# Moving columns of the down and output products read from two runs in turn

## The chip, the core and the metric

The kernel runs on one core of a Trainium2 chip. The time is the device time of one launch in microseconds (us). The core's engines work side by side and wait for each other through semaphores: TensorE (matmuls, PE in the profile; its loads of the stationary operand are PEld), VectorE (DVE), ScalarE (ACT), GpSimd (POOL) and SyncE (SP), which issues nearly all transfers.

## The reference

Two layers over 512 tokens of width 1024. Layer 0 mixes tokens by causal average pooling, layer 1 by stick-breaking attention with 16 heads of 64; each is followed by a squared-ReLU MLP of width 4096, and each block sits between two RMSNorms. Keys and values are projected once, after layer 0.

```python
def sq_relu_mlp(h, w_up, w_down):
    u = jnp.matmul(h, w_up)
    return jnp.matmul(jnp.square(jax.nn.relu(u)), w_down)
...
for layer in range(DEPTH):                      # DEPTH = 2
    h = rms_norm(x, mix_pre_g[layer])
    if layer < N_A:                             # layer 0
        m = pool_mixer(h, pool_w[layer], pool_scale[layer])
    else:                                       # layer 1
        q = ...matmul(h, w_q[j])...
        o = stick_breaking_attention(q, k, v)
        m = jnp.matmul(o..., w_o[j])            # the output projection
    x = x + rms_norm(m, mix_post_g[layer])
    h = rms_norm(x, mlp_pre_g[layer])
    x = x + rms_norm(sq_relu_mlp(h, w_up[layer], w_down[layer]), mlp_post_g[layer])
    if layer == N_A - 1:
        kv = jnp.matmul(rms_norm(x, kv_norm_g), w_kv)...
return x
```

`w_down` (the down projection, 4096 x 1024 in each layer) and `w_o` (the output projection, 1024 x 1024) are the two weights of the change.

## The kernel before

A matmul instruction has a stationary operand of 128 x 128, loaded by an instruction of its own, and a moving operand of 128 rows by up to 512 columns; one result column per moving column goes to a bank of PSUM (128 x 512 float32).

Every dense product is made of three matmuls. Each operand is split into a high part, rounded to the type float32r, and a low part, the remainder (`split`, or `weight` for weights that come from memory; ScalarE makes the high part and VectorE the low one). Then high x high, high x low and low x high are summed in PSUM (`mm3`). In the profile float32r operands of matmuls are listed as f32. The pooling's products (L769, L793) and the transposes on TensorE (L366, L827, L1025) are plain float32, without a split.

Where the products of the change lie:

- The up projection (`up_block`, L654 to L656) has the weights as stationary operand and the 512 tokens' activations, `xnh` and `xnl`, as moving one. Query and key projections go through it as well.
- The down projection has the activations as stationary operand and the weights as moving one, 512 columns at a time, half of the width of 1024. Its rows (4096, as 32 tiles of 128) come in five groups of 2, 3, 3, 3 and 3 pairs of tiles and a rest of 4 tiles.
- A group (class `Seven`) is a 2 x 2 block product done with seven products instead of eight: tokens are halved, rows are taken as even and odd tiles, and the output columns are halved (`NS`: 0 to 511 and 512 to 1023). `right` forms sums and differences of weight quarters on VectorE, in float32 and column by column, and splits them into a tile `w`; `left` does the same for the activations, into a tile `a`. `product` (L543) runs the matmuls, with `a` stationary and `w` moving, and VectorE or ScalarE adds each bank to `y` (L552, L549).
- `contract` multiplies plainly with `mm3` (L293 to L295). It does the rest of 4 tiles (weights named `dn`, or `w` where a pool lends a tile) and the output projection (weights `w`, the last one `h` and `l`; activations `ohl`). Its moving operands are halves of 512 columns too; only for the last 128 tokens of the last layer is the second half cut in two of 256 (`cuts`).
- The value projection (`values`) also uses `mm3`, with 256 moving columns.

The weights lie in memory as 128 x 1024 tiles, `in_wdn` and `in_wo`, arranged by the host program before the launch (`arrays` at the end of the program). The weights of attention are split into parts early and kept in memory (`kept`), to be fetched later.

The order of work: a scheduler places instructions that are not in a hand-made order; in layer 0's mixing, in scores, and in `contract` where a norm follows, the order on TensorE is the order of the code.

Of the kernel before, what the change touches and what calls it, by code (L numbers as in the profile page):

```python
# [15 lines left out]
P = 128  # L16
D = 1024
# [4 lines left out]
NJ = FF // P  # L22
# [6 lines left out]
PAIRS = HEADS // 2  # L29
WINDOWS = (2, 4, 8, 16)  # L30
EPS = 1e-6
TS = [slice(t * P, (t + 1) * P) for t in range(T)]
NS = [slice(0, 512), slice(512, 1024)]
# [38 lines left out]
def trunk(ctx, tc, x, consts, gcol, grow, pw, wup, wdn, wq, wk, wv, wo, out):  # L72
# [14 lines left out]
    def ps():  # L87
        return psum.tile([P, 512], F32, tag="ps", name=name("ps"))
# [145 lines left out]
    def fill(n=1):  # L234
        if gate[0]:
            behind.update(latest)
        for _ in range(n):
            if queue and len(made) < ahead and (queue[0][0][0] != "dn" or dn_pool[0]):
                make()
# [6 lines left out]
    for l in range(2):  # L246
        if l == 1:
            n = len(queue)
# [37 lines left out]
    def rstd(st, col, total=None):  # L286
# [2 lines left out]
        latest["pool"] = nc.gpsimd.tensor_tensor(out=r, in0=total, in1=mhalf, op=ALU.pow)  # L289
        return r  # L290

    def mm3(dst, ah, al, bh, bl, start, stop):
        nc.tensor.matmul(dst, ah, bh, start=start, stop=False)  # L293
        nc.tensor.matmul(dst, ah, bl, start=False, stop=False)  # L294
        nc.tensor.matmul(dst, al, bh, start=False, stop=stop)  # L295
# [9 lines left out]
    class Update:  # L305
# [24 lines left out]
        def product(self, n):  # L330
            return self.beside if n and self.cuts is not NS else self.scaled
# [46 lines left out]
    def contract(lhs, w, y, first, update=None, tiles=range(T), soon=False):  # L378


        last = len(lhs) - 1
        ups = {}
        for t in tiles:
            up = ups[t] = update(t, y[t]) if update is not None else None
            cuts = up.cuts if up is not None else NS
            pds = [ps()[:, : cut.stop - cut.start] for cut in cuts]

            def product(n, cs):
                for c in cs:
                    (lh, ll), (wh, wl) = lhs[c], w[c]  # L390
                    mm3(
                        pds[n], lh[:, TS[t]], ll[:, TS[t]], wh[:, cuts[n]], wl[:, cuts[n]],
                        c == 0, c == last,
                    )

            def evacuate(n):
                part = y[t][:, cuts[n]]
                if first:
                    nc.scalar.copy(part, pds[n])
                else:  # L400
                    nc.vector.tensor_tensor(out=part, in0=pds[n], in1=part, op=ALU.add)
                if up is not None:
                    up.square(n, part, nc.vector if n else nc.gpsimd)

            normed = up is not None and not up.final
            if t == 0:
                product(0, range(last))
                product(1, range(last))
                product(0, [last])
            else:  # L410
                product(0, range(last + 1))
            if normed and t == T - 1 and not soon:
                ups[0].transpose()
            evacuate(0)
            if normed and t > 0:
                ups[t - 1].rstd()
                behind_sum = soon and t == T - 1
                if not behind_sum:
                    ups[t - 1].norm()
            if t == 0:  # L420
                product(1, [last])
            elif normed and t == T - 1:
                product(1, [0])
                ups[1].transpose()
                product(1, range(1, last + 1))
            else:
                product(1, range(last + 1))
                if normed and soon and t == 2:
                    ups[0].transpose()
            evacuate(1)  # L430
            for n in range(2, len(cuts)):
                product(n, range(last + 1))
                evacuate(n)
            if up is None:
                fill()
            else:
                up.add(ups[t - 1].norm if normed and t > 0 and behind_sum else None)
                if normed and t == T - 2:
                    behind.update(latest)
        if normed:  # L440
            ups[T - 1].rstd()
            ups[T - 1].norm()
            for t in (T - 2, T - 1):
                pending[t] = ups[t]
# [4 lines left out]
    class Seven:  # L449
# [84 lines left out]
        def product(self, i, y, first):  # L534
            a, w = self.operands.pop(i)
            at, _, _, tokens, half = self.PRODUCTS[i]
            start = at not in self.banks
            if start:
                self.banks[at] = [ps(), ps()]
            for t, bank in enumerate(self.banks[at]):  # L540
                for q in range(self.n):
                    for k, (x, z) in enumerate(((0, 0), (0, 1), (1, 0))):
                        nc.tensor.matmul(  # L543
                            bank, a[:, x, q, TS[t]], w[:, z, q], start=start and q == 0 and k == 0,
                            stop=q == self.n - 1 and k == 2, skip_group_check=True,
                        )
                part = y[2 * tokens + t][:, NS[half]]
                if first and (tokens, half, t) not in first:
                    nc.scalar.copy(part, bank)  # L549
                    first.add((tokens, half, t))  # L550
                else:
                    nc.vector.tensor_tensor(out=part, in0=bank, in1=part, op=ALU.add)  # L552
# [322 lines left out]
    with tc.tile_pool(name="att", bufs=1, reuse_waits="tile") as ap:  # L875
        att_pool[0] = ap

        def values(u, part):
            if u not in vs:
                w = [get(("v", u, h)) for h in range(2)]  # L880
                vs[u] = w, ap.tile([P, T, 4, 2, HD], F32R, tag="v", bufs=2, name=name("v"))
            w, v = vs[u]
            for s in part:
                need(s)
                pv = ps()
                for k in range(KC):
                    c = slice((k % 4) * 256, (k % 4) * 256 + 256)
                    mm3(
                        pv[:, :256], xnh[:, k, TS[s]], xnl[:, k, TS[s]],
                        w[k // 4][0][:, c], w[k // 4][1][:, c], k == 0, k == KC - 1,  # L890
                    )
                pv4 = pv[:, :256].rearrange("p (h d) -> p h d", h=4)
                nc.scalar.copy(v[:, s, :, 0, :], pv4)
                nc.vector.tensor_tensor(
                    out=v[:, s, :, 1, :], in0=pv4, in1=v[:, s, :, 0, :].bitcast(F32), op=ALU.subtract
                )
# [22 lines left out]
        half = [slice(0, HD), slice(HD, P)]  # L919
# [249 lines left out]
```

## Time and profile before

| | |
|---|---|
| median of 3 timed runs | 946.29 us (946.13 to 946.48) |
| span of the profiled execution, first to last instruction | 944.4 us |
| granted TensorE clock, mean | 0.998 of full speed |
| TensorE busy with matmuls | 935.6 us (99%), 4762 matmuls |
| TensorE busy with loads of stationary tiles | 795.8 us (84%) |
| VectorE, ScalarE, GpSimd busy | 704.5, 566.1, 89.1 us |
| moved by transfers | 169.36 MB, 49.8% of the time of 16 transfer engines |

For the profiled execution the span is the only time that is recorded. The timed runs are 1.7 to 2.1 us above it. A busy time is the time in which at least one instruction of that kind was running; matmuls overlap, so that the mean duration of one is longer than the step from one to the next.

In the order of time: the pooling layer lies up to about 33 us, the first MLP from there to about 366 us, attention with its projections to about 606 us, the second MLP from there to the end. Line numbers are those of the kernel before; in the kernel after, each is 6 higher from `mm3` on.

### The profile page before, as it was taken

How to read it: one execution, taken by the hardware profiler on the slowest of the kernel's cores; microseconds unless marked ns; L12 is line 12 of the kernel's file. 1: busy time of each engine (PE TensorE's matmuls, PEld its weight loads, DVE VectorE, ACT ScalarE, POOL GpSimd, SP SyncE). 2: the span in 40 equal slices, each digit the busy share in tenths (PEclk: the TensorE clock that was granted, in tenths of full speed). 3: DMA queues.
4: the chain of work that ended last, by engine and by line, in shares of the span. 5: the costliest groups of instructions: out<-in, count | busy, mean ns of one | idle time of the engine just before them, and what ended most of it. 6: DMA issues, size and time to landing. Idle time of an engine off the chain costs nothing.

```text
span 944.4 us, 12431 instructions
## 1 busy us (share of the span) xinstructions
PE 935.6 (99%) x4762; PEld 795.8 (84%) x4762; DVE 704.5 (75%) x762; ACT 566.1 (60%) x972; POOL 89.1 (9%) x86
## 2 busy tenths in 40 slices
PE   9999999999999999999999999999999999999997
PEld 7998888888888888988889898898888888888886
DVE  5856797987969756589586887854695876857856
ACT  6658979687874537576647553555544444444632
POOL 2100000000000014000000000311220300403003
PEclk9999999999999999999999999999999999999999
DMA  7444989698683423998625264433414143133102
GB/s 278 170 143 158 340 283 321 234 351 296 235 303 131 155 90 112 359 399 318 238 90 179 90 240 163 156 112 104 164 42 168 58 134 112 45 134 112 47 21 89
DMA packets 46929, 169.36 MB, mean 179 GB/s; under 512 B 4832, under 2 KB 5306, under 8 KB 46870
## 3 DMA queue, kind: packets, MB, share of 16 engines
q1 hardware_dynamic: 46722, 168.55, 49.8%
q8 instruction: 37, 0.61, 0.3%
q14 instruction: 22, 0.18, 0.0%
q10 hardware_dynamic: 148, 0.02, 0.0%
HBM read 128.71 MB, written 39.85 MB: 178 GB/s over the span
## 4 chain that ended last, share of the span: by engine, by line
PE 93%; DVE 3%; DMA 1%; POOL 1%; issue 1%; ACT 1%; POOLq 0%; DVEq 0%; ACTq 0%
PE ps L543 28%; PE ps L655 15%; PE ps L654 15%; PE ps L656 15%; PE ps L293 4%; PE ps L295 4%; PE ps L294 4%; PE ps L976 2%; PE ps L1035 2%; PE ps L1025 2%; PE ps L793 1%; PE ps L769 1%; DMA w<-kept 1%; DVE x L340 1%; PE ps L827 0%
## 5 line engine op out<-in xcount | busy, mean ns | idle before, releaser
L543 PE MATMUL ps<-w,a 128*128 128x512 f32 x1176 | 279.4, 389 | 0.0
L655 PE MATMUL ps<-xnl,w 128*128 128x512 f32 (+1 forms) x712 | 261.8, 368 | 0.1
L654 PE MATMUL ps<-xnh,w 128*128 128x512 f32 (+1 forms) x712 | 261.7, 369 | 0.0
L656 PE MATMUL ps<-xnh,w 128*128 128x512 f32 (+1 forms) x712 | 261.7, 368 | 0.0
L543 PEld LDWEIGHTS ps<-w,a 128*128 128x128 f32 x1176 | 220.8, 188 | 45.8
L655 PEld LDWEIGHTS ps<-xnl,w 128*128 128x128 f32 x712 | 134.3, 189 | 22.3 <-DVE xnl L273 0.5
L656 PEld LDWEIGHTS ps<-xnh,w 128*128 128x128 f32 x712 | 134.2, 189 | 22.1
L654 PEld LDWEIGHTS ps<-xnh,w 128*128 128x128 f32 x712 | 133.6, 189 | 21.9 <-ACT xnh L272 0.2
L552 DVE TENSOR_TENSOR y<-ps,y 128x512 f32<-128x512 f32 x124 | 83.8, 684 | 44.1 <-PE ps L543 44.1
L135 DVE TENSOR_TENSOR w<-raw,w 128x1024 fp32r<-128x1024 f32 x56 | 69.4, 1240 | 62.7 <-ACT w L133 62.6
L133 ACT CAST w<-raw 128x1024 fp32r<-128x1024 f32 x56 | 58.8, 1050 | 79.9 <-PE ps L656 78.2
L328 POOL TENSOR_TENSOR y<-y,grow 128x512 f32<-128x512 f32 x12 | 18.7, 1562 | 576.0 <-ACT xn L276 576.0
L272 ACT CAST w<-e 128x1536 fp32r<-128x1536 f32 (+1 forms) x30 | 41.9, 1397 | 40.0 <-DVE e L516 27.1
L273 DVE TENSOR_TENSOR w<-e,w 128x1536 fp32r<-128x1536 f32 (+1 forms) x30 | 55.6, 1852 | 11.5 <-ACT w L272 11.2
L272 ACT CAST a<-r 128x768 fp32r<-128x768 f32 (+1 forms) x60 | 47.4, 790 | 25.7 <-DVE r L497 12.9
L273 DVE TENSOR_TENSOR a<-r,a 128x768 fp32r<-128x768 f32 (+1 forms) x60 | 59.2, 986 | 0.0
L1007 DVE TENSOR_TENSOR_SCAN e<-u,begin 128x1280 f32<-128x1280 f32 x16 | 45.2, 2822 | 17.4 <-ACT u L1001 16.9
L144 ACT ACTIVATE apart<-apart,gc 128x128 f32<-128x128 f32 (+1 forms) x136 | 43.7, 402 | 0.0
L272 ACT CAST w<-xn 128x1536 fp32r<-128x1536 f32 (+1 forms) x20 | 28.0, 1398 | 25.4 <-PE ps L543 25.4
L273 DVE TENSOR_TENSOR w<-xn,w 128x1536 fp32r<-128x1536 f32 (+1 forms) x20 | 33.0, 1651 | 13.3 <-ACT w L272 13.2
L273 DVE TENSOR_TENSOR w<-w,w 128x1536 fp32r<-128x1536 f32 (+1 forms) x20 | 34.6, 1731 | 9.4 <-ACT w L272 9.4
L272 ACT CAST w<-w 128x1536 fp32r<-128x1536 f32 (+1 forms) x20 | 28.0, 1400 | 21.0 <-PE ps L543 20.9
(151 smaller groups left out, 1418.5 us busy)
## 6 DMA issues: line engine op xcount, KB each, us to landing
w<-kept SPq DMA_DIRECT2D x70, 512.0 KB, 5.1
raw<-in_wup SPq DMA_DIRECT2D x62, 512.0 KB, 4.3
w<-in_wdn SPq DMA_DIRECT2D x8, 1536.0 KB, 7.0
kept<-wx SPq DMA_DIRECT2D x24, 512.0 KB, 4.9
xn<-in_wdn SPq DMA_DIRECT2D x8, 1536.0 KB, 6.5
kept<-apart SPq DMA_DIRECT2D x22, 512.0 KB, 5.0
kept<-xn SPq DMA_DIRECT2D x12, 512.0 KB, 8.1
kept<-spare SPq DMA_DIRECT2D x8, 512.0 KB, 5.3
```

Of the source, the lines that this page charges most:

```text
L133: nc.scalar.copy(hi, raw)
L135: nc.vector.tensor_tensor(out=lo, in0=raw, in1=hi.bitcast(F32), op=ALU.subtract)
L144: nc.scalar.mul(c, c, gc[:, lo + k : lo + k + 1])
L272: latest["act"] = nc.scalar.copy(hi, src)
L273: latest["dve"] = nc.vector.tensor_tensor(out=lo, in0=src, in1=hi.bitcast(F32), op=ALU.subtract)
L293: nc.tensor.matmul(dst, ah, bh, start=start, stop=False)
L543: nc.tensor.matmul(bank, a[:, x, q, TS[t]], w[:, z, q], start=start and q == 0 and k == 0, stop=q == self.n - 1 and k == 2, skip_group_che ...
L552: nc.vector.tensor_tensor(out=part, in0=bank, in1=part, op=ALU.add)
L654: nc.tensor.matmul(pu[:, cols], wh[:, k, :], xnh[:, k, cols], start=k == 0, stop=False)
L655: nc.tensor.matmul(pu[:, cols], wh[:, k, :], xnl[:, k, cols], start=False, stop=False)
L656: nc.tensor.matmul(pu[:, cols], wl[:, k, :], xnh[:, k, cols], start=False, stop=k == KC - 1)
L1007: nc.vector.tensor_tensor_scan(out=e[:, ::-1], data0=u[:, 1:][:, ::-1], data1=begin[:, ::-1], initial=0.0, op0=ALU.mult, op1=ALU.max,)
```

## The change

The host program permutes the columns of `w_down` and `w_o` within each half of 512: first the 256 even columns, then the 256 odd ones. A new helper, `by_twos`, views a half as two runs of 256 columns and takes one column from each in turn: position 0, 256, 1, 257 and so on, which are the columns in their natural order. `product` and `contract` give this view to TensorE as moving operand. So PSUM, and all that follows, holds the same columns as before; neighbouring columns of the moving operand lie 256 elements (1 KB) apart. For a cut of 256 columns the view takes 128 from each run.

Nothing else changes. Each engine has the same instructions in the same order as before, with the moving operand's pattern in the 1572 touched matmuls as the one difference, and each transfer moves the same shape.

```diff
+    def by_twos(w, cut):
+
+        half = w[:, NS[cut.start // 512]].rearrange("p (j i) -> p i j", j=2)
+        lo = cut.start % 512 // 2
+        return half[:, lo : lo + (cut.stop - cut.start) // 2]
+
     def mm3(dst, ah, al, bh, bl, start, stop):
...
                     mm3(
-                        pds[n], lh[:, TS[t]], ll[:, TS[t]], wh[:, cuts[n]], wl[:, cuts[n]],
+                        pds[n], lh[:, TS[t]], ll[:, TS[t]], by_twos(wh, cuts[n]), by_twos(wl, cuts[n]),
                         c == 0, c == last,
                     )
...
                         nc.tensor.matmul(
-                            bank, a[:, x, q, TS[t]], w[:, z, q], start=start and q == 0 and k == 0,
+                            bank, a[:, x, q, TS[t]], by_twos(w[:, z, q], NS[0]), start=start and q == 0 and k == 0,
                             stop=q == self.n - 1 and k == 2, skip_group_check=True,
                         )
...
+    twos = lambda w: w.reshape(*w.shape[:-1], 2, D // 4, 2).swapaxes(-1, -2).reshape(w.shape)
...
-        "wdn": a["w_down"].reshape(2, NJ, P, D),
+        "wdn": twos(a["w_down"].reshape(2, NJ, P, D)),
...
-        "wo": a["w_o"][0].reshape(PAIRS, P, D),
+        "wo": twos(a["w_o"][0].reshape(PAIRS, P, D)),
```

## The prediction

> **What bounds the kernel now.** I read the clock first, then the busy times and the waits, then the chain and the groups by shape, since the change touches only one operand of one kind of instruction. The core's clock, the page's spans, its chain by engine, and all that the trace lists as waits of TensorE:
>
> ```profile
> core 0: 944.4 us, clock 0.998
> span 944.4 us, 12431 instructions
> PE 935.6 (99%) x4762; PEld 795.8 (84%) x4762; DVE 704.5 (75%) x762; ACT 566.1 (60%) x972; POOL 89.1 (9%) x86
> PE 93%; DVE 3%; DMA 1%; POOL 1%; issue 1%; ACT 1%; POOLq 0%; DVEq 0%; ACTq 0%
> PE ps L700 <- POOL warm L662: 1.3, 1, 1.3
> PE ps L293 <- ACT xnh L272: 0.2, 1, 0.2
> ```
>
> The reader is to see a TensorE that never stands still: 935.6 of 944.4 us busy, 1.5 us of waits in all, at a granted clock of 0.998. So the time is a sum over matmuls, and what one matmul takes from its start to the next one's start goes straight into the result. The groups by shape show which are touched (names are output<-moving operand,stationary operand):
>
> ```profile
> L543 PE MATMUL ps<-w,a 128*128 128x512 f32 x1176 | 279.4, 389 | 0.0
> L293 PE MATMUL ps<-dn,sq 128*128 128x512 f32 x60 | 23.5, 392 | 0.0
> L293 PE MATMUL ps<-w,ohl 128*128 128x512 f32 x56 | 21.8, 398 | 0.0
> L293 PE MATMUL ps<-h,ohl 128*128 128x512 f32 x8 | 3.1, 390 | 0.0
> L293 PE MATMUL ps<-dn,sq 128*128 128x256 f32 x8 | 2.3, 282 | 0.0
> ```
>
> L543 is the seven-product part of both down projections. L293 is the first of the three matmuls of `mm3`; L294 and L295 have one for each of it. So 1176 + 3 x (60 + 56 + 8) = 1548 matmuls of 512 columns and 3 x 8 = 24 of 256 take their moving columns in the new way: 1572 matmuls, 1548 x 512 + 24 x 256 = 798,720 columns. The 389 ns of a row is no price, since matmuls overlap; the price is the step from start to start, which the chain of waits gives (start, us, what). Below are a run of L543, one of L793 (plain float32, 128x256) and one of L1025 (plain float32 transposes, 128 columns), then two rows of the timeline with 22 steps between them, all of 256 columns in the value projection, which the change leaves alone:
>
> ```profile
> 331.00 8.16 PE ps L543 x36
> ...
> 29.40 3.46 PE ps L793 x16
> ...
> 572.85 0.66 PE ps L1025 x6
> ...
> 366.86 0.28 PE L295 MATMUL ps<-w,xnl 128*128 128x256 f32 x1
> ...
> 369.50 0.28 PE L654 MATMUL ps<-xnh,w 128*128 128x256 f32 x1
> ```
>
> A step of 512 columns is 8.16 / 36 = 226.7 ns, one of 256 is 2.64 / 22 = 120.0 ns. The difference, 106.7 ns over 256 columns, is 0.4168 ns a column; what is left, 226.7 - 213.4 = 13.3 ns, is a fixed part of each matmul. The plain float32 rows give 3.46 / 16 = 216.3 ns for 256 columns and 0.66 / 6 = 110 ns for 128: 0.83 ns a column, twice as much, and a fixed part of only 216.3 - 2 x 0.4168 x 256 = 2.9 ns. Both kinds load a 128x128 float32 stationary tile for each matmul, so the load alone doesn't explain the 13.3 ns:
>
> ```profile
> L543 PEld LDWEIGHTS ps<-w,a 128*128 128x128 f32 x1176 | 220.8, 188 | 45.8
> L793 PEld LDWEIGHTS ps<-pw,yt 128*128 128x128 f32 x64 | 11.8, 190 | 1.9 <-issue 0.5
> ```
>
> **The change part by part.** *The moving operand.* It goes from one run of 512 elements to 256 pairs whose halves lie 1 KB apart. Nothing in this trace reads a moving operand in that manner, so the step of a touched matmul has to be bounded.
>
> From below: the whole fixed part goes. That is 13.3 ns x 1572 = 20.9 us, and 946.3 - 20.9 = 925.4 us. Less isn't excluded by any mechanism, but no row has a column cheaper than 0.4168 ns.
>
> From above: each column costs what it costs in the nearest slower rows, L793's, 0.83 ns. Then 0.4168 ns is added for each of 798,720 columns, 332.9 us, and 1279.2 us come out; 1262.8 us if the fixed part shrinks too, as it has in those rows.
>
> Which value? What sets fast from slow in the rows is the pace at which one run is read. At 0.4168 ns a column of one run, a matmul carries 13.3 ns beside its columns; at half that pace along a run, it carries 2.9 ns. After the change each of the two runs is read at half the pace, as L793's is, while together they would still give a column every 0.4168 ns. By that likeness a touched matmul of 512 columns takes 213.4 + 2.9 = 216.3 ns, and one of 256 takes 109.6 ns: 10.4 ns less each, 10.4 x 1572 = 16.4 us. I take this end, since L793 is the one group in which the fixed part is seen to be small with the same stationary loads; it is a likeness and no proof, because L793 differs also in how TensorE handles plain float32, and the chances below say so.
>
> [...]
>
> *The layout of the two weight tensors.* Nothing at run time: the columns are permuted within each half of 512 before the launch, the transfers have the same shapes and sizes, and the sums and differences of weight halves go column by column, so their instructions are the same. Order and number of instructions on all five engines stay as they are, SP's transfers among them.
>
> *What the shorter steps meet.* 588 of L543's matmuls lie in each layer, 6.1 us of gain in each of two stretches. The two stretches between the first and the last products of seven:
>
> ```profile
> core 0: us, PE busy (x) PEld busy (x) DVE busy (x) ACT busy (x) POOL busy (x), PEclk, DMA share, GB/s
> 62.90:338.00 275.10, 275.10 (x1215) 227.87 (x1214) 222.09 (x214) 208.97 (x347) 0.00 (x0) 1.00 0.70 249
> 607.80:920.00 312.20, 312.20 (x1463) 261.89 (x1463) 220.35 (x201) 152.63 (x186) 47.46 (x22) 1.00 0.30 101
> ```
>
> In the first VectorE is busy 222.1 of 275.1 us; in 269 it would be 83%, the DMA share 72%. The waits there point at TensorE, not from it:
>
> ```profile
> ACT w L272 <- PE ps L543: 59.1, 38, 2.2
> DVE y L552 <- PE ps L543: 44.1, 36, 4.2
> DVE e L516 <- DMA xn<-in_wdn: 10.1, 8, 2.1
> PEld ps L294 <- DMA w<-kept: 0.2, 1, 0.2
> ```
>
> VectorE and ScalarE wait 103 us for the touched matmuls, so they follow a faster TensorE at once. The cover that could go is the last row's: the kept output-projection weights land 0.2 us late once. But the slots they land in are freed by TensorE, so most of the transfer moves forward with it; I cost this at nothing, and at some 2 us if it stays where it is. The end of the chain stays as it is:
>
> ```profile
> 934.75 0.70 DVE y L401
> ...
> 936.34 1.57 POOL y L328
> ...
> 941.10 0.40 DVE x L340
> ```
>
> The last matmul's result is taken at 934.75 us, and what follows does not read the weights.
>
> *The sum.* The profiled execution's span is 944.4 us, 1.9 us under the median of the timed runs (946.29); that remainder lies outside the span and does not change. 944.4 - 16.4 = 928.0 us of span, and 946.3 - 16.4 = 929.9 us of time; I say 930.
>
> **The rivals.**
>
> *The column rate falls to half (slower).* Place: the reader of TensorE's moving operand, in all 1572 matmuls. If what it fetches from SBUF at a time serves only neighbouring columns, then alternating between two places makes each column a fetch of its own, and the rate is that of L793's rows. Price: 1262.8 to 1279.2 us, as above. It decides as soon as it adds more than 10.4 ns to a matmul, that is 25 column times in 512, one lost for every 20 columns. For it: all moving operands of the trace are contiguous, so nothing shows that two places can be kept open. Against it: nothing in the trace either; it is the open question. A cost between, some columns delayed and others not, would end between 948 and 1262 us.
>
> [...]
>
> *Nothing changes.* The 13.3 ns may belong to the exchange of the stationary tile at full column rate: in L793 that exchange has twice the time per column to hide in. If two runs are read as well as one, 226.7 ns stay, and the time is 946.3 us. For it: 512 and 256 columns show the same fixed part, as an exchange would. Against it: L793's 2.9 ns with the same loads.
>
> *Half the gain.* Only one of two starts of a run is hidden: 5.2 ns x 1572 = 8.2 us, 938 us.
>
> **How the numbers follow.** The full gain (near 930) gets 0.40 and the half gain 0.05; nothing changes 0.17; half the column rate 0.27; a cost in between 0.11. So faster 0.45, same 0.17, slower 0.38, where same means within 0.2% or 1.9 us, about what a measurement of this kernel can tell from no change. The likeliest case is the full gain, 930 us; its own range is 925 to 938. Cases of both signs hold most of the chance, so the whole range has to reach from 925 (the fixed part gone) to 1279 (each column doubled, the fixed part kept): leaving out the half rate would already leave out more than 2 in 10.
>
> **What would show it.** In the changed kernel, a run of 36 L543 matmuls (L549 there) should take 7.8 us in the chain instead of 8.16, with TensorE still at 99% and the up projections still at 226.7 ns. If such a run takes 8.16 us, the fixed part was not the reading's. If it takes about 15.5, the column rate has halved; then VectorE's and ScalarE's waits for L549 should grow to some hundred us, with their busy time unchanged. The forecast is wrong also if the steps shrink and the time does not: then a wait of TensorE for weights or operands must appear in its list, which has 1.5 us now.

## The result and the profile after

The changed kernel takes 932.55 us (median of 4 runs, 932.35 to 934.18) against 946.23 us of the kernel before on the same chip: a ratio of 0.9856, 95% interval 0.9842 to 0.9870. That is 13.7 us less, where the likeliest case of the forecast, 930 us, had 16.4 us less. The profiled execution took 932.74 us with a span of 930.9 us; the span of before was 944.4 us, so 13.5 us went.

From the page of the changed kernel, the span, the busy times and the chain by engine:

```profile
span 930.9 us, 12431 instructions
PE 921.5 (99%) x4762; PEld 797.6 (86%) x4762; DVE 703.6 (76%) x762; ACT 565.0 (61%) x972; POOL 91.7 (10%) x86
PE 93%; DVE 2%; DMA 1%; issue 1%; POOL 1%; ACT 1%; POOLq 0%; DVEq 0%; SPq 0%; ACTq 0%
```

TensorE is still the bound at 99%, and VectorE's and ScalarE's work is what it was (704.5 and 566.1 us before). All that went, went from TensorE's steps. The chain of waits of the changed kernel (start, us, what) has the run of 36 products that the prediction read at 331.00 us, and the end of the kernel:

```profile
326.58 7.77 PE ps L549 x36
...
921.22 0.70 DVE y L407
...
927.56 0.40 DVE x L346
```

7.77 / 36 = 215.8 ns a step, where 226.7 ns stood before. Two rows of its timeline, 16 steps apart in the last piece of 256 columns:

```profile
921.80 0.28 PE L300 MATMUL ps<-dn,sq 128*128 128x256 f32 x1
...
923.58 0.28 PE L301 MATMUL ps<-dn,sq 128*128 128x256 f32 x1
```

1.78 / 16 = 111 ns, 120.0 before. The groups by shape show what moved the other way (busy us, mean ns of one):

```profile
L549 PE MATMUL ps<-w,a 128*128 128x512 f32 x1176 | 266.6, 379 | 0.0
L660 PE MATMUL ps<-xnh,w 128*128 128x512 f32 x568 | 222.9, 392 | 0.0
L662 PE MATMUL ps<-xnh,w 128*128 128x512 f32 x568 | 222.1, 391 | 0.0
L661 PE MATMUL ps<-xnl,w 128*128 128x512 f32 x568 | 221.5, 390 | 0.0
```

The seven products fell from 279.4 to 266.6 us. The up projections, which nobody touched, rose from 221.8, 221.3 and 221.1 us (L654, L656, L655 before) to these values, 2.3 us together. Where that sits is seen in one block of 24 of them between touched products; the timeline of the changed kernel gives its start and the start of what follows:

```profile
81.84 0.40 PE L660 MATMUL ps<-xnh,w 128*128 128x512 f32 x1
...
87.31 0.59 PE L549 MATMUL ps<-w,a 128*128 128x512 f32 x2
```

5.47 us for 24 steps, where 24 steps of 226.7 ns are 5.44. From start to start, the first six steps of this block take 231 to 236 ns but for one of 228, and from the seventh on each takes 226 or 227.

Summed over all steps from one start to the next in the two traces, the seven products gave 12.8 us, the products of `contract` 4.2 us, the up projections took back 2.9 us, and the rest changed by 0.6 us: 12.8 + 4.2 - 2.9 - 0.6 = 13.5 us, the difference of the spans. No wait took the gain; the trace lists 2.2 us of them for TensorE, 0.7 us more than before:

```profile
PE ps L706 <- POOL warm L668: 1.3, 1, 1.3
PE ps L661 <- DVE xnl L273: 0.5, 1, 0.5
PE ps L299 <- ACT xnh L272: 0.2, 1, 0.2
PE ps L300 <- DMA w<-kept: 0.2, 1, 0.2
```

### The profile page after: what moved, and what is told of

Its sections match the earlier page's. It is cut to its first block, busy times and chain, and to the rows that moved or that the text cites. A ratio compares the mean times of both kernels' runs of the same rounds, so it can differ in the third digit from the quotient of the medians.

```text
span 930.9 us, 12431 instructions
## 1 busy us (share of the span) xinstructions
PE 921.5 (99%) x4762; PEld 797.6 (86%) x4762; DVE 703.6 (76%) x762; ACT 565.0 (61%) x972; POOL 91.7 (10%) x86
## 4 chain that ended last, share of the span: by engine, by line
PE 93%; DVE 2%; DMA 1%; issue 1%; POOL 1%; ACT 1%; POOLq 0%; DVEq 0%; SPq 0%; ACTq 0%
PE ps L549 27%; PE ps L660 15%; PE ps L661 15%; PE ps L662 15%; PE ps L300 4%; PE ps L301 4%; PE ps L299 4%; PE ps L982 2%; PE ps L1031 2%; PE ps L799 2%; PE ps L1041 1%; DMA w<-kept 1%; PE ps L775 1%; DVE x L346 1%; PE ps L706 0%
## 5 line engine op out<-in xcount | busy, mean ns | idle before, releaser
L549 PE MATMUL ps<-w,a 128*128 128x512 f32 x1176 | 266.6, 379 | 0.0
L558 DVE TENSOR_TENSOR y<-ps,y 128x512 f32<-128x512 f32 x124 | 83.9, 685 | 36.9 <-PE ps L549 36.8
L273 DVE TENSOR_TENSOR w<-e,w 128x1536 fp32r<-128x1536 f32 (+1 forms) x30 | 52.5, 1749 | 11.0 <-ACT w L272 10.8
L581 ACT ACTIVATE r<-ps 128x512 f32<-128x512 f32 x56 | 33.1, 591 | 9.5 <-PE ps L662 9.5
```

The lines of the kernel that those rows point to most:

```text
L273: latest["dve"] = nc.vector.tensor_tensor(out=lo, in0=src, in1=hi.bitcast(F32), op=ALU.subtract)
L549: nc.tensor.matmul(bank, a[:, x, q, TS[t]], by_twos(w[:, z, q], NS[0]), start=start and q == 0 and k == 0, stop=q == self.n - 1 and k == 2 ...
```

## The experiments

**Many patterns side by side.** The size of the step was right, but a likeness to plain float32 is no cause. A kernel that holds nothing but groups of 36 matmuls measures the step for one pattern of moving columns after the other (`h` is 512 columns of a float32r tile `m`, `a` the stationary operand; some of the groups are shown):

```diff
+    twos = lambda v, j: v.rearrange("p (j i) -> p i j", j=j)
...
+        ("one", h, a, P),
+        ("turn", twos(h, 2), a, P),
+        ("four", twos(h, 4), a, P),
...
+        ("lines", h.rearrange("p (b j i) -> p b i j", j=2, i=4), a, P),
+        ("inline", h.rearrange("p (b j i) -> p b i j", j=2, i=2), a, P),
...
+        ("swapped", h.rearrange("p (j i) -> p j i", j=2)[:, ::-1], a, P),
...
+        ("steptwo", h.rearrange("p (i j) -> p j i", j=2), a, P),
...
+            for i in range(36):
...
+                nc.tensor.matmul(dst, s[:, at : at + n], v, start=i == 0, stop=i == 35)
```

> This kernel computes nothing of the trunk: it copies x to the output and runs 26 groups of 36 matmuls, each matmul with its own 128x128 stationary tile, each group with its own way of taking the moving columns. Read: the step from start to start. Groups of 512 float32r columns unless said. one, swapped (two runs one after the other), descend, offset, again; turn, four, eight (2, 4, 8 runs in turn, 1 KB, 512 B, 256 B apart); sixteen, lines, inline (two neighbouring runs of 16, 4, 2 columns in turn); pairs and quads (2 or 4 columns from each of two runs in turn); steptwo and stepfour (every second or fourth column of one stretch); narrow and slim (64 or 32 stationary columns); less (384) and half (256 columns); brief (bfloat16). Pace theory (the pace along one run decides): one, swapped, descend, offset 226.7 ns; turn, four, eight, sixteen, lines, pairs, quads 216; steptwo and stepfour, one stretch at twice and four times the pace, over 226.7; narrow and slim 226.7. Form theory (any pattern that is not one contiguous run will do): swapped, steptwo, stepfour and inline 216 too. Load theory (the moving reads lose one column time for each 16 bytes of the stationary tile's rows, 32 for 128 columns, unless the pattern lets them pass): narrow 220, slim 216.7 at one run; narrowturn 216; brief in one run half of the surplus or less, up to 220. All: less 173 and lessturn 162 to 163, half 120 and halfturn 112.

From the chain of waits of this kernel; each row is one group:

```profile
19.83 8.16 PE one L105 x36
27.99 7.77 PE turn L105 x36
35.76 10.20 PE four L105 x36
45.96 17.61 PE eight L105 x36
63.57 7.77 PE sixteen L105 x36
71.34 7.77 PE lines L105 x36
79.11 8.16 PE inline L105 x36
87.28 12.23 PE pairs L105 x36
99.51 9.01 PE quads L105 x36
108.51 8.20 PE swapped L105 x36
125.12 16.24 PE steptwo L105 x36
157.97 8.28 PE narrow L105 x36
166.25 7.77 PE narrowturn L105 x36
182.35 6.25 PE less L105 x36
188.60 5.85 PE lessturn L105 x36
194.45 4.32 PE half L105 x36
198.77 4.02 PE halfturn L105 x36
202.79 7.79 PE brief L105 x36
210.57 17.44 PE briefturn L105 x36
```

Divide by 36. One run and two in turn come out as in the whole kernel, 226.7 and 215.8 ns, with nothing else running. The pace theory, the prediction's, falls: four runs in turn, each read at a quarter of the pace, take 283 ns, eight 489. The form theory falls: `inline` and `swapped` are no single run either, and take 227 and 228. The load theory falls: with 64 stationary columns instead of 128 one run takes 230 ns, not less, and two in turn (`narrowturn`) 216 as before. Of the smaller sizes, 384 columns take 173.6 in one run (`less`) and 162.5 ns in turn (`lessturn`), 256 take 120.0 and 111.7 (`half`, `halfturn`). So beside 0.4168 ns a column one run takes a fixed 13.3 to 13.6 ns at every size, and two in turn 2.4 to 2.5 ns at 384 and 512 columns; at 256 it is 5.0.

bfloat16 is another matter: `brief` (one run) needs 216 ns as it is, and in turn 484. So the rival that the column rate falls to half, given 0.27, names something that exists: `steptwo` (451 ns) has it, and the bfloat16 turn loses somewhat more. It only doesn't exist for this pattern in this type.

**A theory of places.** What the 216 ns patterns have in common: look at the columns at even places alone, and at those at odd places alone. A line is from here on a name for four float32r columns that lie side by side in the tile, counted off from its start. In `turn`, `sixteen` and `lines`, each of the two sequences takes 4 columns in a row from the same line; in `one`, `inline` and `swapped` 2; in `steptwo` 1. The idea, the author's guess from these times: the more columns in a row each sequence takes from one line, the shorter the step, 216 ns at 4, 227 to 228 at 2, 451 at 1. A second set of groups was built to part this (`places` below) from a rival (`neighbours`) by which the next line of each run has to lie beside the last one (`hop`: 4 columns of a line from each run in turn, then on by 64 bytes; `same`: each of 256 columns twice):

```diff
+    words = lambda v, j, c: v.rearrange("p (j i c) -> p i c j", j=j, c=c)
...
+        ("same", h[:, :256].rearrange("p (i o) -> p i o", o=1).broadcast_to((P, 256, 2)), a, P),
+        ("wide", words(m[:, :1024], 2, 2)[:, :, 0], a, P),
+        ("wider", words(m, 2, 4)[:, :, 0], a, P),
+        ("hop", words(m, 2, 16)[:, :, :4], a, P),
+        ("skip", words(m, 2, 8)[:, :, :2], a, P),
...
+        ("plainturn", twos(raw[0][:, :256], 2), raw[2], P),
+        ("mixed", None, a, P),
```

> Groups of 36 matmuls again, and nothing of the trunk. After the first groups the pace theory cannot stand (four runs in turn took 283 ns, eight 487). [...] same (each of 256 columns twice): places 216. wide (two runs in turn, each at step two): places 226.7; neighbours 216 or 450. wider (each at step four): places 450 to 461. hop (4 columns of a line from each run in turn, then on by 64 bytes): places 216; neighbours over 226.7. skip (2 of a line, then on by 32 bytes): places 226.7 to 250. slanted (second run begins 8 bytes later in its line): 216. shiftone (both runs 4 bytes later): 216 to 237. offtwo, offfour, offeight (one run, 8, 16, 32 bytes later): 226.7, offtwo up to 237. blocks (16 columns of each run in turn): places 227 to 232. briefpairs, briefquads (bfloat16, 2 or 4 columns of each run in turn): places 216 for pairs if a 4-byte word is a place, else over 300. plain, plainturn (float32, 256 columns): 216. mixed (one run and two in turn by turns): 221.3 if the fixed part belongs to each matmul alone; up to 226 if a change of pattern costs something.

From its chain of waits (plain float32 has two matmuls for each of the program's, so 72):

```profile
35.97 7.77 PE same L102 x36
43.74 8.18 PE wide L102 x36
51.92 16.31 PE wider L102 x36
68.24 7.77 PE hop L102 x36
76.01 8.32 PE skip L102 x36
92.13 7.80 PE shiftone L102 x36
116.67 8.40 PE offeight L102 x36
125.06 8.64 PE blocks L102 x36
141.49 9.76 PE briefpairs L102 x36
159.41 15.54 PE plain L102 x72
174.95 19.67 PE plainturn L102 x72
194.62 8.04 PE mixed L102 x36
```

`same`, `wide`, `wider`, `hop` and `skip` came as the theory of places has it: 216, 227, 453, 216 and 231 ns; `shiftone` (both runs 4 bytes later) stays at 217. `hop` at 216 excludes that the next line has to be the neighbour. Its misses: `blocks` 240 (227 to 232 expected), `offeight`, one run that begins 32 bytes later, 233 instead of 226.7, `briefpairs` 271, and `plainturn` 273 instead of 216. The first groups speak against it too: in `four` and `pairs` each of the two sequences changes its line at every column, as in `steptwo`, and yet they take 283 and 340 ns, not 451; `quads` has 2 in a row and takes 250, not 227. So the theory put the second set of float32r groups in the right order, but as a rule it is too simple for four runs, for where a run begins and for jumps, and it says nothing of bfloat16 and plain float32. What in TensorE parts the fast patterns from the slow ones no run shows; why two runs in turn are faster stays open.

`mixed` bears on the term that the prediction lacked. By turns, one run and two in turn take 223.3 ns on average (8.04 / 36), not the mean of 221.3. Step by step, the matmuls in turn stay at 215 ns, and those of one run take 229 to 235 ns (231.6 on average, 2 x 223.3 - 215) instead of 226.7, much as the first steps of the changed kernel's block at 81.84 us (231 to 236 but for one): one run pays for the change of pattern, some 5 ns, and two runs in turn do not.

**The up projections in turn as well.** If this is right, the other large moving operand should gain too, and the slower first steps of its blocks should go. Here the runs are 64 tokens long, and the order is made by the transposes ahead:

```diff
+    parted = ident.rearrange("p (i j) -> p j i", j=2)
...
-                    nc.tensor.transpose(pt[:, TS[c]], self.xn[:, k * P : (k + 1) * P], ident)
+                    nc.tensor.transpose(
+                        pt[:, TS[c]], self.xn[:, k * P : (k + 1) * P], ident if self.gpre is None else parted
+                    )
...
+        def moving(x, k):
+            v = x[:, k, cols]
+            return v.rearrange("p (t j i) -> p t i j", j=2, i=P // 2) if turn else v
...
-            nc.tensor.matmul(pu[:, cols], wh[:, k, :], xnh[:, k, cols], start=k == 0, stop=False)
+            nc.tensor.matmul(pu[:, cols], wh[:, k, :], moving(xnh, k), start=k == 0, stop=False)
```

> Both MLPs' up projections take their moving columns in turn as well: within each 128 tokens two runs of 64, the tokens being written in that order by the transposes ahead. 1344 matmuls of 512 columns and 384 of 256. Pace and form theory: 10.9 ns and 8.3 ns less each, 14.6 + 3.2 us, and the slower first steps of each block of up projections after touched matmuls (some 2.1 us in the two MLPs) go too: 912.6 us, 20 us less than the changed kernel. Rival (the gain needs runs far apart, or belongs to the weights as moving operand): 932 to 933 us. Second rival (the transposes with a permuted identity lose their pace): up to 2 us of that gain lost, 914 to 915 us.

Measured: 913.24 us (5 runs) against 947.04 us of before, ratio 0.9645, 0.9632 to 0.9658. From the groups by shape of this kernel:

```profile
L667 PE MATMUL ps<-xnh,w 128*128 128x512 f32 x568 | 217.3, 383 | 0.0
L669 PE MATMUL ps<-xnh,w 128*128 128x512 f32 x568 | 216.8, 382 | 0.0
L668 PE MATMUL ps<-xnl,w 128*128 128x512 f32 x568 | 216.6, 381 | 0.0
```

Each fell by some 5 us below the changed kernel's; a busy row understates it, since its matmuls (383 ns each) overlap those of its two neighbours. The span fell from 930.9 to 911.0 us. From start to start, all up projections together take 20.0 us less than in the changed kernel, and those of the MLPs with 512 columns are at 215 or 216 ns (two of 1344 at 218 and 219), the first steps of a block among them. The chain has such a block behind touched products:

```profile
84.96 2.59 PE ps L552 x12
87.55 0.22 PE ps L667
87.77 0.22 PE ps L668
87.98 0.22 PE ps L669
88.20 0.22 PE ps L667
88.41 0.22 PE ps L668
```

Its first four steps take 0.86 us, 215 ns each. The forecast of 20 us came out to within 1 us. So the slower first steps belong to one run read after another pattern, and they go when the up projections are taken in turn too. The touched products never had them: in the changed kernel they are at 215 or 216 ns from the first step behind an up projection.

**Four runs in place of two.** The groups say that the pattern, not the idea of taking turns, makes the gain. In the whole kernel:

```diff
-        half = w[:, NS[cut.start // 512]].rearrange("p (j i) -> p i j", j=2)
-        lo = cut.start % 512 // 2
+        half = w[:, NS[cut.start // 512]].rearrange("p (j i) -> p i j", j=4)
+        lo = cut.start % 512 // 4
...
-    twos = lambda w: w.reshape(*w.shape[:-1], 2, D // 4, 2).swapaxes(-1, -2).reshape(w.shape)
+    twos = lambda w: w.reshape(*w.shape[:-1], 2, D // 8, 4).swapaxes(-1, -2).reshape(w.shape)
```

> The changed kernel with four runs in turn in place of two: down and output weights laid out as the four classes of columns by 4. Places theory: each reader alternates between two lines, as in the group of four runs, 283.3 ns for 512 columns, 56.6 ns more than one run before: 1548 x 56.6 = 87.6 us over the kernel before, 1034 us. The pace theory would have said 930 to 933 us.

Measured: 1031.98 us (4 runs), ratio 1.0898, 1.0883 to 1.0913. Its span and a run of its products in the chain:

```profile
span 1030.0 us, 12431 instructions
...
313.46 10.17 PE ps L549 x36
```

10.17 / 36 = 282.5 ns. The 283.3 ns of the expectation are the group `four`, 10.20 / 36; that readers alternate between lines no run shows. The step measured by itself foretold the kernel's time within 2 us of 85.

**Two smaller products more.** To the kernel with the up projections in turn, the value projection and the product of attention weights and values are added:

```diff
-                        w[k // 4][0][:, c], w[k // 4][1][:, c], k == 0, k == KC - 1,
+                        *(x[:, c].rearrange("p (j i) -> p i j", j=2) for x in w[k // 4]), k == 0, k == KC - 1,
...
-                        nc.tensor.transpose(pt[:, c : c + P], w[:, at : at + P], ident)
+                        nc.tensor.transpose(pt[:, c : c + P], w[:, at : at + P], parted)
...
-                        parts[s][n][:, c : c + S - s * P],
+                        parts[s][n][:, c : c + S - s * P].rearrange("p (t j i) -> p t i j", j=2, i=P // 2),
...
-    wv = blocks(a["w_kv"][:, D:], 256).reshape(4, P, 2, D).transpose(0, 2, 1, 3)
+    wv = blocks(a["w_kv"][:, D:], 256)
+    wv = wv.reshape(*wv.shape[:-1], P, 2).swapaxes(-1, -2).reshape(4, P, 2, D).transpose(0, 2, 1, 3)
```

> The kernel of e2 with two more products in turn: the value projection (384 matmuls of 256 columns, the value weights laid out as evens then odds of each 256) and the products of the attention weights with the values (32 matmuls each of 512, 384, 256 and 128 columns, permuted by the transposes). Theory: 8.3 ns less for each of 256, 10.9 for each of 384 and 512, nothing for 128: 3.2 + 0.7 + 0.3 us, 909 us. Rival (attention waits for other engines or for kept weights, and takes nothing): 912 to 913.5 us.

Measured: 910.71 us (5 runs) against 946.97, ratio 0.9617, 0.9604 to 0.9630. The gain is there, but short of the forecast by 1.7 us. From start to start, against the trace of the kernel without this edit, the value projection gave 3.1 us (its busy times fell from 108.9 to 105.9 us) and the products of 384 and 512 columns 0.9 us (24.0 to 23.2 us busy), about as forecast; those of 256 columns gave nothing of their 0.3 us (9.2 to 9.0 us busy), and the attention's transposes lost 1.2 us. The transposes have become dearer; their row in the kernel without this edit, then in the one with it:

```profile
L1038 PE MATMUL ps<-ident,w 128*128 128x128 f32 x160 | 20.4, 273 | 0.0
```

```profile
L1038 PE MATMUL ps<-ident,w 128*128 128x128 f32 x160 | 21.4, 277 | 0.0
```

From start to start a transpose takes 114 ns (the median) through the strided identity and 109 through the plain one: here plain float32 as moving operand loses 5 ns in 128 columns by a step of two. A last kernel brings the permuted identity from memory as it is needed:

```diff
-    parted = ident.rearrange("p (i j) -> p j i", j=2)
+    parted = keep.tile([P, P], F32, tag="parted", name="parted")
...
+        nc.sync.dma_start(parted, consts[:, 4 * (P + BORDER) + P :])
...
-    return np.concatenate([*first, *border, eye], axis=1).astype(np.float32)
+    return np.concatenate([*first, *border, eye, eye[:, ::2], eye[:, 1::2]], axis=1).astype(np.float32)
```

> The kernel of e4, but the permuted identity of the transposes lies in memory in that order and is loaded by a transfer of 64 KB of its own, in place of the strided view of the identity. In e4 a plain float32 transpose of 128 columns through that view took about 114 ns from start to start, against 109 through the identity as it lies. Theory: 192 transposes x 5 ns, 1.0 us less than e4 on the same chip, 909.7 us. Rival (the transposes wait for other things, or the extra transfer delays the start): 910.7 us or more.

Measured: 910.09 us (5 runs) against 946.64, ratio 0.9613, 0.9600 to 0.9626. The interval overlaps that of the kernel without this edit almost wholly, so that a gain of 1 us in the time is neither shown nor excluded. In the two traces the transposes are back at 109 ns and take 28.1 us together from start to start, against 29.1 us (34.3 against 35.3 us busy). Both kernels beat the one before by 3.8 to 3.9% and the changed one by some 2.4 to 2.5%.

## Why the prediction was right or wrong, step by step

- *The bound.* Right: a sum over TensorE's steps, and nothing else changed.
- *The step of a touched matmul.* Right in size: 216.3 ns was forecast, 215.8 measured, 2.4 ns beside the columns in place of 2.9. For 256 columns 109.6 was forecast and 111 to 112 measured, 5.0 ns beside the columns.
- *Why.* Wrong, and the size was right by luck in part. The pace along one run does not decide: four runs in turn (283 ns) refute it, and so does plain float32 in turn (273 ns), the very kind from which the likeness was drawn. The number taken from L793 and the measured one lie close together, 2.9 and 2.4 ns beside the columns; that they have one cause was not shown. A likeness between two groups that differ in more than one thing set the right value and would have set the same value for four runs, where it fails by 67 ns.
- *What else the shorter steps meet.* Mis-sized: the 16.4 us counted touched matmuls alone. These gave 12.8 + 4.2 = 17.0 us, but the untouched up projections lost 2.9 us, a term of the sum that the prediction put at nothing; its sign that they stay at 226.7 ns fails for the first steps of a block. The trace of before could not show this in the MLPs, where all matmuls have one pattern, but it shows it in attention. There a block of query or key projections behind transposes starts slowly too (the rows are 9 and 10 steps apart):

```profile
431.31 0.39 PE L654 MATMUL ps<-xnh,w 128*128 128x512 f32 x1
...
433.39 0.39 PE L654 MATMUL ps<-xnh,w 128*128 128x512 f32 x1
...
435.65 0.39 PE L655 MATMUL ps<-xnl,w 128*128 128x512 f32 x1
```

  2.08 / 9 = 231 ns a step, then 2.26 / 10 = 226 ns. A term for these steps could have been read there.
- *No wait takes the gain.* Right. VectorE and ScalarE waited 50.6 + 36.8 = 87.4 us for the touched matmuls, against 103.2 us before, so they followed at once:

```profile
ACT w L272 <- PE ps L549: 50.6, 36, 2.0
DVE y L558 <- PE ps L549: 36.8, 32, 3.7
```

- *The late weights.* TensorE waited 0.2 us for `kept` at a matmul and 0.6 us at a load, against 0.2 us at a load before; the feared 2 us did not come.
- *Nothing changes, half the gain.* The step of 215.8 ns excludes both. TensorE loads as many stationary tiles as before (4762), so the 10.9 of the 13.3 ns that went were not the price of exchanging them.
- *Half the column rate.* It did not happen, and the chance of 0.27 was fair on what the trace showed: all its moving operands are contiguous. With neighbouring columns 1 KB apart the step is 215.8 ns. About half the rate came with another pattern, every second column of one stretch (`steptwo`, 451 ns). The theory of places fits most of the float32r groups, but not `four`, `pairs` and `quads` (283, 340 and 250 ns).

## What to carry to other kernels

Where TensorE is the bound, take the step from start to start for two column counts and split it into a price per column and a fixed part; a fixed part above that of another kind of matmul (here 13.3 ns against 2.9) is time to look for. Try patterns of the moving operand in a kernel of nothing but matmuls before changing a layout, since the next pattern over cost more here: four runs 25% (283 against 226.7 ns), pairs 50% (340), bfloat16 in turn 124% (484 against 216). And count the matmuls that lie beside the changed ones.

## What the runs showed of the hardware that was not expected

- Float32r moving columns from two runs in turn: 215.8 ns for 512, against 226.7 from one run; the 1 KB between neighbours costs nothing beside 16 bytes (`lines`, 215.8). Runs 256 bytes apart in the up projections do as well (215 or 216). With 16 columns from each run in turn it is 240, with 2 from each 340, from four runs in turn 283, every second column of one stretch 451.
- The fixed part of one run does not depend on the number of columns (13.3 ns at 256 and 512, 13.6 at 384), but it does on where the run begins: 32 bytes later it is 20 ns (`offeight`, 233.3 a step). Why is open.
- Turning the same pattern on plain float32 (216 to 273 ns for 256 columns) or bfloat16 (216 to 484 for 512) makes it slower.
- A matmul of one run behind one of two runs in turn takes some 5 ns longer (231.6 ns against 226.7), the other way round nothing is lost (215 or 216 ns from the first step), and most blocks of up projections in the MLPs need six to ten steps until their step is back at 226 or 227 ns. What settles there is open too.
